# Two experts' inputs gathered at once, and the S5 tables' second part placed later, in a two-layer trunk on one core

## The chip, the core and the metric

The kernel runs on one core of a Trainium2 chip. The metric is the device time of one execution in microseconds, the median of several runs. TensorE (PE) multiplies matrices, VectorE (DVE), ScalarE (ACT) and GpSimd (POOL) work element by element, SyncE (SP) issues most DMA transfers. Each engine takes its instructions in the order in which they were written for it, and waits on semaphores for the others.

## The reference

Two layers over 256 latent and 256 context tokens of width 1024. Each layer has four parallel mixers (gated DeltaNet, S5, HGRN2, retention) between one input and one output projection; then layer 0 has a dense SwiGLU, layer 1 a mixture of eight experts of which each token takes two.

```python
def _swiglu(h, w1, w3, w2):
    return (jax.nn.silu(h @ w1) * (h @ w3)) @ w2

def _moe_swiglu(h, router, w1, w3, w2):
    ...
    logits = _f32(tok @ router)
    top_val, top_idx = lax.top_k(logits, TOP_K)
    gates = jax.nn.softmax(top_val, axis=-1)
    ...
    def expert_block(args):
        xblk, e = args
        return (jax.nn.silu(xblk @ w1[e]) * (xblk @ w3[e])) @ w2[e]
    yb = lax.map(expert_block, (xb, block_expert)).reshape(n_rows, -1)
    ...

def reference(x, c, ctx, ...):
    for layer in range(DEPTH):
        ...                      # the four mixers, w_out, layer norm
        x = _layer_norm(DEEPNORM_ALPHA * x + gt2 * ffn(x * (1.0 + sc2) + sh2), ln_g[layer, 1], ln_b[layer, 1])
```

The S5 mixer is a diagonal complex state space: lam_bar is raised to powers, and products of the powers with B and C make tables with which the scan is done in chunks.

## The kernel before

All is float32. A product of two float32 matrices is done as three products of parts (high times high, low times high, high times low): `whi` or `mhi` is a weight's high part, cast by ACT (L390), `wlo` or `mlo` the rest, subtracted by DVE (L305); `xh` and `xl` are the same of an input. Products are recorded at L373, the line of a helper.

**Order.** A framework places the instructions of each engine by a simulated timeline and by priorities. `context("B")` or `"A"` picks a scratch ring (k2B, k2A, k2P; each a ring of 128x512 tiles) and a priority; `high_priority(-2000)` moves work behind all other ready work. So the order is not written out, and an edit in one place may shift it in others.

**Stages.** By the trace's time: layer 0's start and S5 tables (0 to 140 us), its mixers (to 515), output projection and layer 1's S5 tables (to 610), the dense FFN (to 985), layer 1's mixers and the routing (to 1424), the experts (to 2456), the last norm.

**S5 tables.** `s5_tables` makes the powers and the state tables; `s5_out_tables` (L1343) the output tables: eight tiles Y of 128x512 a layer, each by two multiplications and a subtraction on DVE and one store by SP to a scratch in HBM. In layer 0 it is called in order, in layer 1 with priority -2000 beside the tables and the norm.

**Dense FFN.** A loop over f of 128-row pieces of the hidden width, with weights loaded by SP in tiles `wraw` of 128x1024.

**Experts.** `experts` (L1900) runs 8 experts x 7 steps. A step's `up` (L1824) takes four units, each a load `mraw` of 1 MB (128x2048) by SP, a cast `mhi` by ACT and a subtraction `mlo` by DVE, and does 48 products of 512 columns into two banks `psh`; SiLU and a multiplication make g (in k2P). `down` (L1844), one step later, transposes g (four transposes, L1848), splits it into `e_gh` and `e_gl`, and takes two more units for 24 products into `psy`. `mraw` has RAW = 8 buffers, `mhi` and `mlo` three each. That makes 8 x 7 x 6 = 336 units. After an expert's last step `scatter` adds its result to the tokens by products with `e_back`, in the next expert's first step. A loop for overflowing experts is built, but has no iterations here.

**The gather.** `gather` (L1765) makes the input of one expert: DVE compares positions with an index row to make `e_sel` (two tiles of 128x128 with one 1 per column), PE transposes these into `e_back`, and 32 products (8 pieces of the width, times two token halves, times high and low part `m_nh`, `m_nl`) select the expert's 128 tokens, 128 columns each. DVE scales and shifts by the modulation (L323), ACT makes `e_xh`, DVE `e_xl`. It is called at the start for expert 0 and in each expert's fifth step (c == 4) for the next.

## Time and profile before

| | us |
|---|---|
| median of 3 runs | 2485.07 (2484.03 to 2487.42) |
| the profiled execution | 2472.9 |
| its span, first to last instruction | 2470.8 |
| TensorE busy | 2262.0 (92%), mean granted clock 0.935 |
| DVE busy | 1735.4 (70%) |
| ACT busy | 1278.3 (52%) |
| POOL busy | 234.8 (10%) |
| read from HBM | 509.23 MB |

Busy times are of one execution. Products of TensorE overlap in the records, so their own durations are longer than the distance at which they start; where a cost is worked out, it is the distance of starts that counts. A table by stage gives, for each stretch, the length, the busy time and count of each engine (PE, PEld for weight loads, DVE, ACT, POOL), the granted clock of TensorE as a share of 2.4 GHz, the DMA's busy share and its GB/s.

### The profile page before, as it was taken

How to read it: one execution, taken by the hardware profiler on the slowest of the kernel's cores; microseconds unless marked ns; L12 is line 12 of the kernel's file. 1: busy time of each engine (PE TensorE's matmuls, PEld its weight loads, DVE VectorE, ACT ScalarE, POOL GpSimd, SP SyncE). 2: the span in 40 equal slices, each digit the busy share in tenths (PEclk: the TensorE clock that was granted, in tenths of full speed). 3: DMA queues.
4: the chain of work that ended last, by engine and by line, in shares of the span. 5: the costliest groups of instructions: out<-in, count | busy, mean ns of one | idle time of the engine just before them, and what ended most of it. 6: DMA issues, size and time to landing. Idle time of an engine off the chain costs nothing. (4 is left out here: it accounts for less than half of the span.)

```text
span 2470.8 us, 33235 instructions
## 1 busy us (share of the span) xinstructions
PE 2262.0 (92%) x12928; PEld 1777.8 (72%) x12928; DVE 1735.4 (70%) x2558; ACT 1278.3 (52%) x1483; POOL 234.8 (10%) x238
## 2 busy tenths in 40 slices
PE   4989989789999999799858799999999999999997
PEld 2767755565888887478747478787878788788885
DVE  8574657787444322464767599888888988889887
ACT  2634423325444422643524357676767667677775
POOL 0111331000111100002331000000000000010000
PEclk8989997789999999889978799999999999999998
DMA  7622144227223323742320669898998989899994
GB/s 296 220 90 81 61 163 137 90 89 273 94 95 102 124 94 131 241 147 81 106 75 27 227 246 353 323 347 335 344 347 336 353 320 363 318 369 341 364 356 164
DMA packets 123667, 532.75 MB, mean 216 GB/s; under 512 B 26096, under 2 KB 37360, under 8 KB 80112
## 3 DMA queue, kind: packets, MB, share of 16 engines
q1 hardware_dynamic: 96624, 511.74, 56.7%
q10 hardware_dynamic: 26880, 18.82, 2.6%
q8 instruction: 104, 1.70, 0.3%
q14 instruction: 59, 0.48, 0.1%
HBM read 509.23 MB, written 21.28 MB: 215 GB/s over the span
## 5 line engine op out<-in xcount | busy, mean ns | idle before, releaser
L305 DVE TENSOR_TENSOR mlo<-mraw,mhi 128x2048 fp32r<-128x2048 f32 x336 | 776.1, 2323 | 107.5 <-ACT mhi L390 105.8
L390 ACT CAST mhi<-mraw 128x2048 fp32r<-128x2048 f32 x336 | 639.1, 1906 | 216.3 <-PE psh L373 131.9
L373 PE MATMUL psh<-mlo,e_xh 128*128 128x512 f32 x896 | 357.9, 399 | 6.3 <-DVE mlo L305 6.3
L373 PE MATMUL psh<-mhi,e_xh 128*128 128x512 f32 x896 | 351.5, 395 | 7.8 <-ACT mhi L390 7.8
L373 PE MATMUL psh<-mhi,e_xl 128*128 128x512 f32 x896 | 351.6, 393 | 0.0
L390 ACT CAST whi<-wraw 128x1024 fp32r<-128x1024 f32 x142 | 145.9, 1028 | 375.0 <-PE psacc L373 346.8
L373 PE MATMUL psacc<-xh,whi 128*128 128x512 f32 (+2 forms) x784 | 314.1, 401 | 18.7 <-ACT k2P L329 8.4
L373 PE MATMUL psacc<-xl,whi 128*128 128x512 f32 (+2 forms) x784 | 309.3, 395 | 0.2 <-DVE xl L305 0.2
L373 PE MATMUL psacc<-xh,wlo 128*128 128x512 f32 (+2 forms) x784 | 306.8, 392 | 0.5 <-DVE wlo L305 0.4
L305 DVE TENSOR_TENSOR wlo<-wraw,whi 128x1024 fp32r<-128x1024 f32 x142 | 172.1, 1212 | 167.5 <-ACT whi L390 165.4
L373 PEld LDWEIGHTS psh<-mhi,e_xh 128*128 128x128 f32 x896 | 169.8, 189 | 46.1 <-ACT mhi L390 8.9
L373 PEld LDWEIGHTS psh<-mlo,e_xh 128*128 128x128 f32 x896 | 170.2, 190 | 43.2 <-DVE mlo L305 8.4
L373 PEld LDWEIGHTS psh<-mhi,e_xl 128*128 128x128 f32 x896 | 169.9, 190 | 34.4
L373 PEld LDWEIGHTS psacc<-xh,whi 128*128 128x128 f32 (+1 forms) x784 | 152.4, 195 | 56.3 <-ACT k2P L329 9.6
L373 PE MATMUL psy<-mlo,e_gh 128*128 128x512 f32 x448 | 176.9, 396 | 1.4 <-DVE mlo L305 1.4
L373 PEld LDWEIGHTS psacc<-xl,whi 128*128 128x128 f32 (+1 forms) x784 | 152.2, 194 | 34.3 <-issue 4.3
L373 PEld LDWEIGHTS psacc<-xh,wlo 128*128 128x128 f32 (+1 forms) x784 | 151.4, 193 | 35.0 <-issue 4.0
L373 PE MATMUL psy<-mhi,e_gl 128*128 128x512 f32 x448 | 173.7, 391 | 0.0
L373 PE MATMUL psy<-mhi,e_gh 128*128 128x512 f32 x448 | 159.9, 394 | 0.0
L305 POOL TENSOR_TENSOR e_xl<-k2B,e_xh 128x512 fp32r<-128x512 f32 x16 | 31.3, 1966 | 1024.5 <-ACT e_xh L1872 1024.5
L373 PEld LDWEIGHTS psy<-mlo,e_gh 128*128 128x128 f32 x448 | 84.4, 188 | 20.1 <-DVE mlo L305 2.9
L373 PEld LDWEIGHTS psy<-mhi,e_gh 128*128 128x128 f32 x448 | 84.3, 188 | 20.0 <-ACT e_gh L1851 1.5
(533 smaller groups left out, 3454.9 us busy)
## 6 DMA issues: line engine op xcount, KB each, us to landing
mraw<-in_moe_w_dram SPq DMA_DIRECT2D x336, 1024.0 KB, 6.5
wraw<-in_ada_w_dram SPq DMA_DIRECT2D x80, 512.0 KB, 4.4
wraw<-in_ffn_w_dram SPq DMA_DIRECT2D x60, 512.0 KB, 3.4
wraw<-in_w_feat_dram SPq DMA_DIRECT2D x44, 512.0 KB, 3.6
sraw<-in_ada_w_dram SPq DMA_DIRECT2D x16, 512.0 KB, 9.8
wraw<-in_w_out_dram SPq DMA_DIRECT2D x16, 512.0 KB, 3.9
wraw<-in_w_tok_dram SPq DMA_DIRECT2D x12, 512.0 KB, 3.4
s5c<-s5Y SPq DMA_DIRECT2D x16, 256.0 KB, 4.1
```

The lines of the kernel that those rows point to most:

```text
L305: (eng or self.V).tensor_tensor(out=out, in0=a, in1=b, op=op)
L373: self.T.matmul(out, lhsT, rhs, start=start, stop=stop, **k)
L390: self.S.copy(hi, raw)
```

## The change

Four things.

- `RAW` is 7 instead of 8.
- `s5_out_tables` is a generator that stops after each Y. Layer 0 runs it through after the first part's pool is left, in a pool of its own (`tabo`); layer 1 keeps it as `self.later` and takes one Y at each f > 2 of the FFN, with scratch from k2A.
- `gather` takes two experts: `e_sel` is two tiles of 128x256, a piece of the width is done for both at once, 32 products of 256 columns, two pieces to a bank instead of four. Scaling is done for both at once (128x256), ACT's copy and DVE's subtraction for each by itself. It is called at the start for experts 0 and 1, and in the fifth step of experts 1, 3 and 5 for the next two. `e_x` has three buffers, `e_back` three, `e_sel` one.
- `moe_begin` loads the norm's rows in halves into k2P by SP's queue instead of whole into an idle `e_x` by ACT's; its four operations become eight of half the width.

```diff
--- before.py
+++ after.py
@@ -229,7 +229,7 @@
 
 
 class Trunk:
-    RAW = 8
+    RAW = 7
 
     def __init__(self, ctx, tc, A, out, cat, pat, dbg=None):
         self.ctx, self.tc, self.nc = ctx, tc, tc.nc
@@ -1340,7 +1340,7 @@
         self.s5y2 = LC, Call
         return sr, sw, scm, sT
 
-    def s5_out_tables(self, scm):
+    def s5_out_tables(self, scm, ypool, cx):
 
         LC, Call = self.s5y2
         sh = [P, 4, 16, 8]
@@ -1349,13 +1349,14 @@
             lc = tuple(LC[:, c, gs, None, :].to_broadcast(sh) for c in range(2))
             cb = tuple(Call[:, c, gs, :, None].to_broadcast(sh) for c in range(3))
             for c, (a, b) in enumerate(((0, 1), (2, 0))):
-                Y = self.t("s5Y", [4, 16, 8])
-                with self.context("B"):
+                Y = self.t("s5Y", [4, 16, 8], pool=ypool)
+                with self.context(cx):
                     tmp = self.s2().rearrange("p (g h i) -> p g h i", g=4, h=16)
                 self.mul(Y, lc[0], cb[a])
                 self.mul(tmp, lc[1], cb[b])
                 self.sub(Y, Y, tmp)
                 self.nc.sync.dma_start(scm[g0 // 4][:, c * 512:c * 512 + 512], Y.rearrange("p g h i -> p (g h i)"))
+                yield
 
 
     def s5_phases(self, res):
@@ -1677,6 +1678,8 @@
             self.product([[A["ffn_w3"][f]]], self.xh, self.xl, NTOK, lambda i, acc: self.mul(h, h, acc))
             self.S.copy(gh[f], h)
             self.sub(gl[f], h, gh[f].bitcast(F32), eng=self.G)
+            if f > 2:
+                next(self.later, None)
         res = self.big.tile([P, KT, NTOK], F32, tag="xl", name=self.name("fres"))
         self.load_res(res, xt, (0, 1))
         pm = self.ps()
@@ -1762,38 +1765,40 @@
         self.nover = mt("nov", 1, dt=I32)
         self.V.tensor_copy(self.nover, cnt)
 
-    def gather(self, pos):
-
-
-        sel = self.t("e_sel", [2, P], F32R, bufs=2)
+    def gather(self, *pos):
+
+
+        n = len(pos)
+        sel = self.t("e_sel", [2, 2 * P], F32R)
         for b in range(2):
-            self.ts(sel[:, b], self.C("iota"), pos[b], ALU.is_equal)
+            for e in range(n):
+                self.ts(sel[:, b, e * P:(e + 1) * P], self.C("iota"), pos[e][b], ALU.is_equal)
         self32 = sel.bitcast(F32)
-        pt = self.ps()
-        for b in range(2):
-            self.T.transpose(pt[:, b * P:(b + 1) * P], self32[:, b], self.ident)
-        back = self.t("e_back", [2, P], F32R, bufs=2)
-        self.act(back.rearrange("p b t -> p (b t)"), pt[:, :256], AF.Copy)
-
-        if not self.ex[self.exi]:
-            self.ex[self.exi] = [self.t(f"e_x{c}{self.exi}", [KT, P], F32R) for c in "hl"]
-        xh, xl = self.ex[self.exi]
-        self.exi = 1 - self.exi
+        out = []
+        for e in range(n):
+            pt = self.ps()
+            for b in range(2):
+                self.T.transpose(pt[:, b * P:(b + 1) * P], self32[:, b, e * P:(e + 1) * P], self.ident)
+            back = self.t("e_back", [2, P], F32R, bufs=3)
+            self.act(back.rearrange("p b t -> p (b t)"), pt[:, :256], AF.Copy)
+            out.append((back, *(self.t("e_x" + c, [KT, P], F32R, bufs=3) for c in "hl")))
+
         A, B = self.AB[:, 0, 1], self.AB[:, 1, 1]
-        for k0 in range(0, KT, 4):
-            px = self.ps()
-            for k in range(4):
+        for k0 in range(0, KT, 2):
+            px = self.ps()[:, :2 * n * P].rearrange("p (k t) -> p k t", k=2)
+            for k in range(2):
                 for i, (nn, b) in enumerate((nn, b) for b in range(2) for nn in (self.nh, self.nl)):
-                    self.mm(px[:, k * P:(k + 1) * P], nn[:, b, (k0 + k) * P:(k0 + k + 1) * P], sel[:, b],
+                    self.mm(px[:, k], nn[:, b, (k0 + k) * P:(k0 + k + 1) * P], sel[:, b, :n * P],
                             start=(i == 0), stop=(i == 3))
             with self.context("B"):
-                x = self.s2().rearrange("p (k t) -> p k t", k=4)
-            for k in range(4):
-                self.ts(x[:, k], px[:, k * P:(k + 1) * P], A[:, k0 + k:k0 + k + 1], ALU.mult,
-                        B[:, k0 + k:k0 + k + 1], ALU.add)
-            self.S.copy(xh[:, k0:k0 + 4], x)
-            self.sub(xl[:, k0:k0 + 4], x, xh.bitcast(F32)[:, k0:k0 + 4])
-        return back, xh, xl
+                x = self.s2()[:, :2 * n * P].rearrange("p (k t) -> p k t", k=2)
+            for k in range(2):
+                self.ts(x[:, k], px[:, k], A[:, k0 + k:k0 + k + 1], ALU.mult, B[:, k0 + k:k0 + k + 1], ALU.add)
+            for e, (_, xh, xl) in enumerate(out):
+                xe = x[:, :, e * P:(e + 1) * P]
+                self.S.copy(xh[:, k0:k0 + 2], xe)
+                self.sub(xl[:, k0:k0 + 2], xe, xh.bitcast(F32)[:, k0:k0 + 2])
+        return out
 
     def raw_unit(self, src):
 
@@ -1884,18 +1889,21 @@
 
     def moe_begin(self):
 
-        rows = [self.t(f"e_x{c}1", [D]) for c in "hl"]
-        for j, nm in enumerate(("ln_g", "ln_b")):
-            self.nc.scalar.dma_start(rows[j], self.A[nm][1, 0:1, :].to_broadcast([P, D]))
 
         f = lambda t: t.bitcast(F32)
         one = f(self.t("e_gl", [4, P], F32R, bufs=2))[:, 0, 0:1]
         self.V.memset(one, 1.0)
         self.stt(self.macc, f(self.nh), one, f(self.nl), ALU.mult, ALU.add)
-        for b in range(2):
-            m = self.macc[:, b]
-            self.stt(m, m, ALPHA, rows[0], ALU.mult, ALU.mult)
-            self.stt(m, rows[1], ALPHA, m, ALU.mult, ALU.add)
+        for h in range(2):
+            sl = slice(h * 512, h * 512 + 512)
+            with self.context("P"):
+                g, s = self.s2(), self.s2()
+            for row, nm in ((g, "ln_g"), (s, "ln_b")):
+                self.nc.sync.dma_start(row, self.A[nm][1, 0:1, sl].to_broadcast([P, 512]))
+            for b in range(2):
+                m = self.macc[:, b, sl]
+                self.stt(m, m, ALPHA, g, ALU.mult, ALU.mult)
+                self.stt(m, s, ALPHA, m, ALU.mult, ALU.add)
 
     def experts(self, jobs, first=False):
 
@@ -1906,8 +1914,7 @@
         with self.tc.high_priority(-500):
             early = [self.unit(src, 4) for src in self.up_srcs(jobs[0][0], 0)[:3]]
         parts = self.up_parts(jobs[0][0], 0, 3)
-        self.ex, self.exi = [None, None], 0
-        x = {0: self.gather(jobs[0][1])}
+        x = dict(enumerate(self.gather(*(j[1] for j in jobs[:2]))))
         y, g, back = {}, {}, None
         for i in range(len(steps) + 1):
             if i < len(steps):
@@ -1915,8 +1922,8 @@
                 if i > 0:
                     parts = self.up_parts(jobs[n][0], c)
                 g[i] = self.up(chain(early if i == 0 else (), parts), x[n])
-                if c == NC - 3 and n + 1 < len(jobs):
-                    x[n + 1] = self.gather(jobs[n + 1][1])
+                if c == NC - 3 and n % 2 and n + 1 < len(jobs):
+                    x.update(enumerate(self.gather(*(j[1] for j in jobs[n + 1:n + 3])), n + 1))
             if i < 4 and first:
                 (self.route_gates, self.route_over, lambda: None, self.moe_begin)[i]()
             if back:
@@ -2011,9 +2018,11 @@
             self.enter("tab", "right")
             tables = self.s5_tables(l, y)
             self.leave("tab")
-            self.mx = y
-            self.s5_out_tables(tables[2])
-            self.leave("taby", "start")
+
+            y = self.enter("tabo", "right")
+            for _ in self.s5_out_tables(tables[2], y, "B"):
+                pass
+            self.leave("tabo", "taby", "start")
         self.enter("sP", "left")
         self.s5_begin(l, tables)
         self.enter("sW", "left")
@@ -2100,9 +2109,7 @@
         with self.context("B"):
             tables = self.s5_tables(1, y)
         self.leave("tab")
-        self.mx = y
-        with self.tc.high_priority(-2000):
-            self.s5_out_tables(tables[2])
+        self.later = self.s5_out_tables(tables[2], y, "A")
         for p in (0, 1):
             self.ada(1, p)
         self.enter("l1", "right")
```

Where instructions move, two places. DVE at layer 0's start, where the input's low part `xl` is made for the first projection. Before:

```order
L305 TENSOR_TENSOR s5Y_1139<-s5LC_834,s5C_700 128x512
L305 TENSOR_TENSOR s5res_768<-s5res_768,s5wtm_858 128x16x16
L305 TENSOR_TENSOR xl_196<-sx_200,xh_195 128x512
L305 TENSOR_TENSOR s5Y_1139<-s5Y_1139,k2B_1140 128x512
L305 TENSOR_TENSOR s5wtm_858<-s5res_768,s5wc_861 128x256
L305 TENSOR_TENSOR xl_196<-sx_200,xh_195 128x512
L305 TENSOR_TENSOR xl_196<-sx_210,xh_195 128x512
L305 TENSOR_TENSOR k2B_1158<-s5LC_834,s5C_700 128x512
L305 TENSOR_TENSOR xl_196<-sx_210,xh_195 128x512
L305 TENSOR_TENSOR s5res_768<-s5res_768,s5wtm_858 128x16x16
```

And now, from the same `xl` on:

```order
L305 TENSOR_TENSOR xl_196<-sx_200,xh_195 128x512 x2
L305 TENSOR_TENSOR xl_196<-sx_210,xh_195 128x512 x2
L305 TENSOR_TENSOR xl_196<-sx_220,xh_195 128x512 x2
L305 TENSOR_TENSOR xl_196<-sx_230,xh_195 128x512 x2
L305 TENSOR_TENSOR rlg_1434<-exp_1437,exi_1438 128x8
L321 TENSOR_SCALAR rlg_1434<-rlg_1434 128x8
L305 TENSOR_TENSOR wlo_319<-wraw_317,whi_320 128x1024
L305 TENSOR_TENSOR wlo_366<-wraw_364,whi_367 128x1024
L305 TENSOR_TENSOR s5Y_1130<-s5LC_834,s5C_700 128x512
```

The operations on s5Y and its scratch k2B stood between those on xl; now the first follows the weights' second wlo.

PE at the third change of expert (from the third to the fourth expert); psh is the fourth expert's first steps, psy the third expert's last and the fourth's first `down`, psA with k2P the transposes of g. Before:

```order
L1848 MATMUL psA_14645<-consts_74,k2P_14494 128x128 x4
L373 MATMUL psh_14690<-mhi_14694,e_xh_1958_12209 128x512
L373 MATMUL psy_2432_14643<-mhi_14657,e_gh_14650 128x512
L373 MATMUL psy_2432_14643<-mlo_14656,e_gh_14650 128x512
L373 MATMUL psy_2433_14644<-mhi_14657,e_gh_14650 128x512
L373 MATMUL psy_2433_14644<-mlo_14656,e_gh_14650 128x512
L1848 MATMUL psA_14767<-consts_74,k2P_14624 128x128 x4
L373 MATMUL psh_14690<-mlo_14693,e_xh_1958_12209 128x512
L373 MATMUL psh_14690<-mhi_14694,e_xl_1959_12210 128x512
L373 MATMUL psh_14690<-mhi_14694,e_xh_1958_12209 128x512
L373 MATMUL psh_14690<-mlo_14693,e_xh_1958_12209 128x512
```

And now:

```order
L373 MATMUL psy_2437_14594<-mlo_14606,e_gh_14600 128x512
L373 MATMUL psy_2437_14594<-mhi_14607,e_gl_14601 128x512
L373 MATMUL psy_2436_14593<-mhi_14625,e_gh_14600 128x512
L373 MATMUL psy_2437_14594<-mhi_14625,e_gh_14600 128x512
L1853 MATMUL psA_14717<-consts_74,k2P_14574 128x128 x4
L373 MATMUL psh_14640<-mhi_14644,e_xh_13135 128x512
L373 MATMUL psy_2436_14593<-mlo_14624,e_gh_14600 128x512
L373 MATMUL psy_2436_14593<-mhi_14625,e_gl_14601 128x512
L373 MATMUL psy_2437_14594<-mlo_14624,e_gh_14600 128x512
L373 MATMUL psy_2437_14594<-mhi_14625,e_gl_14601 128x512
L373 MATMUL psy_2436_14593<-mhi_14625,e_gh_14600 128x512
```

Before, both groups of transposes come within six rows, and 20 psy products of the first `down` follow after eleven of psh; now the psy products stand ahead of and around the second transposes.

## Rows read from the trace of the kernel before

**Rows 1.** The page's part 1, whole span: engine, busy us, share, instructions.

```profile
PE 2262.0 (92%) x12928; PEld 1777.8 (72%) x12928; DVE 1735.4 (70%) x2558; ACT 1278.3 (52%) x1483; POOL 234.8 (10%) x238
```

**Rows 2.** Table by stage, experts; columns: stretch, length, busy (count) per engine, clock, DMA, GB/s.

```profile
1420.00:1440.00 20.00, 17.40 (x79) 15.64 (x79) 16.67 (x95) 5.53 (x6) 0.00 (x0) 0.74 0.15 53
1440.00:1460.00 20.00, 20.00 (x91) 16.52 (x91) 17.94 (x11) 15.91 (x11) 0.00 (x0) 1.00 0.92 346
...
1480.00:1500.00 20.00, 19.99 (x103) 16.70 (x103) 20.00 (x22) 13.12 (x11) 0.00 (x0) 1.00 0.83 296
...
1580.00:1600.00 20.00, 16.91 (x65) 12.78 (x64) 14.53 (x11) 9.70 (x8) 0.00 (x0) 0.83 0.65 239
1700.00:1720.00 20.00, 16.36 (x73) 12.63 (x72) 18.46 (x14) 10.28 (x10) 3.16 (x2) 1.00 0.90 340
1840.00:1860.00 20.00, 16.88 (x62) 13.00 (x63) 13.85 (x10) 9.97 (x8) 0.00 (x0) 0.83 0.65 242
1960.00:1980.00 20.00, 17.37 (x67) 13.05 (x65) 17.79 (x13) 9.70 (x8) 3.15 (x2) 0.83 0.88 310
2100.00:2120.00 20.00, 16.56 (x73) 12.76 (x73) 15.10 (x12) 11.41 (x9) 0.00 (x0) 1.00 0.74 274
2220.00:2240.00 20.00, 19.74 (x90) 16.02 (x90) 19.70 (x14) 13.37 (x10) 3.65 (x2) 1.00 0.87 321
```

**Rows 3.** Timeline of PE at the first change of expert: start, duration, operation, idle before.

```profile
1580.18 0.60 PE L1848 MATMUL psA<-consts,k2P 128*128 128x128 f32 x4
1582.33 0.51 PE L373 MATMUL psh<-mhi,e_xh 128*128 128x512 f32 x1 [1.55 <-ACT mhi L390]
```

**Rows 4.** Waits, 1576 to 1600: engine and line, releaser: us, times, longest.

```profile
ACT mhi L390 <- PE psh L373: 7.8, 3, 5.1
```

**Rows 5.** Timelines of PE: first gather, second gather, a projection of 256 columns.

```profile
1425.29 0.41 PE L373 MATMUL psA<-e_sel,m_nl 128*128 128x128 f32 x1
...
1428.49 0.41 PE L373 MATMUL psA<-e_sel,m_nh 128*128 128x128 f32 x1
...
1485.83 0.27 PE L373 MATMUL psA<-e_sel,m_nh 128*128 128x128 f32 x1
1485.94 0.27 PE L373 MATMUL psA<-e_sel,m_nl 128*128 128x128 f32 x1
...
204.00 0.28 PE L373 MATMUL psacc<-whi,xl 128*128 128x256 f32 x1
204.12 0.28 PE L373 MATMUL psacc<-whi,xh 128*128 128x256 f32 x1
```

**Rows 6.** Timelines of DVE: the first gather, and the modulation of layer 0.

```profile
1428.31 1.36 DVE L323 TENSOR_SCALAR k2B<-psA,lnAB 128x128 f32<-128x128 f32 x4 [0.53 <-PE psA L373]
...
1430.36 0.69 DVE L305 TENSOR_TENSOR e_xl<-k2B,e_xh 128x512 fp32r<-128x512 f32 x1
...
60.38 2.66 DVE L323 TENSOR_SCALAR sx<-sx,sc1p,mods 128x256 f32<-128x256 f32 x8
```

**Rows 7.** Table by stage for layer 0's start, and the tile s5Y: count: minimum/median/maximum ns.

```profile
20.00:40.00 20.00, 6.28 (x41) 3.17 (x34) 19.83 (x114) 3.17 (x4) 0.00 (x0) 0.68 1.03 402
...
120.00:140.00 20.00, 10.22 (x44) 8.20 (x44) 17.39 (x23) 10.37 (x20) 0.00 (x0) 0.83 0.28 93
...
L305 DVE TENSOR_TENSOR s5Y<-s5LC,s5C x16: 680/684/1252, 26.2 to 596.9; 128x512 f32<-128x512 f32 x16
```

**Rows 8.** Timeline of PE at the hole in layer 0.

```profile
131.41 0.40 PE L373 MATMUL psacc<-xh,wlo 128*128 128x512 f32 x1
143.20 2.08 PE L373 MATMUL psP<-k2P,consts 128*128 128x512 f32 x2 [11.39 <-ACT k2P L329]
```

**Rows 9.** Table by stage: layer 1's table stretch, and the dense FFN.

```profile
540.00:560.00 20.00, 20.00 (x95) 15.96 (x95) 20.00 (x67) 6.09 (x12) 0.00 (x0) 1.00 0.30 104
...
620.00:720.00 100.00, 100.00 (x442) 82.81 (x442) 42.57 (x47) 43.41 (x57) 16.35 (x9) 1.00 0.31 97
```

**Rows 10.** The page's part 6: DMA issues, count, KB each, us to landing.

```profile
mraw<-in_moe_w_dram SPq DMA_DIRECT2D x336, 1024.0 KB, 6.5
```

## The prediction

> **What bounds the kernel now.** I read the page's busy shares first, then tables by stage, then the order of events at the places that the diff touches. TensorE is busy 2262.0 of 2470.8 us [rows 1], so the question at each stage is what keeps TensorE from work, or how much work it has. The experts' stage (1424 to 2456 us) is TensorE's in its steady stretches: 20.00 of 20 us busy with some 90 products, VectorE just behind it at 17.94 [rows 2]. Five of the seven changes from one expert to the next break this: the windows from 1580, 1700, 1840, 1960 and 2100 hold 65, 73, 62, 67 and 73 products. The sixth (2220) holds 90, so the stall is no necessity. The timeline of the first shows why [rows 3]: four transposes, 1.55 us of waiting for ACT's mhi, one product of psh, four of psy, four transposes, and a wait for the next unit. ACT itself had waited up to 5.1 us for TensorE's psh [rows 4]: mhi and mlo have three buffers, and a new unit is cast only when an old one has been used up.
>
> In layer 0, DVE is full at 20 to 40 us (19.83 of 20), and TensorE has a hole at 120 to 140 (10.22 of 20) [rows 7]: it waits 11.39 us for ACT's k2P in front of one psP product [rows 8]. In layer 1's table stretch both TensorE and DVE are full; in the FFN only TensorE is, DVE 42.57 of 100 [rows 9].
>
> **The gather.** Before, each expert takes 32 products of 128 columns. At full clock they start 0.11 us apart; in the first gather, in a window with a mean granted clock of 0.74 [rows 2], 15 of them span 3.20 us, 0.213 each [rows 5]. So 32 x 0.213 + 7 x 32 x 0.11 = 6.8 + 24.6 = 31.4 us. After, a pair takes 32 products of 256 columns, four times in all. No gather of 256 columns is in the trace; the projections have 256-column products of the same kinds, 0.12 apart [rows 5]. Bounds: 0.12 (the projection's) and 0.22 (twice the 128-column start). I take 0.12, a product of that size, and for the first pair at low clock twice it, as the 128-column rows have it: 32 x 0.24 + 3 x 32 x 0.12 = 7.7 + 11.5 = 19.2. That is **-12 us**; at 0.22 it is 32 x 0.44 + 96 x 0.22 = 35.2, a loss of 4.
>
> What goes with it on DVE: before, per expert and per half of the k range, four scalings (1.36) and one subtraction (0.69) [rows 6], so 4.1 per expert, 8.2 a pair. After, a pair has eight scalings of 128x256 (2.66 for eight [rows 6]) and eight subtractions of 128x256, between half of 0.69 and the whole of it, 2.8 to 5.5. So 5.5 to 8.2, not more than before in sum, but in one step instead of two, and DVE was full at 20.00 of 20 in the stretch with one gather [rows 2]. That puts up to 4 us more on DVE in each of three steps, and one such excess ahead of the first expert's products, half of which the three mhi/mlo buffers and the step's slack should take: **+3 us** (0 to +12). moe_begin's four operations become eight of half the size, with no gather beside them any more: 0.
>
> The Trainium skill ("TensorE: Matmul & The Clock Gate", section "Back-to-back issue gap") gives N/2.4 + 2.5 ns as the gap of a single product, so 56 and 109 ns, by which two of 128 columns cost what one of 256 does and the gather would save 0.3 us (an estimate from that page). The rows speak against it, 0.11 and 0.12. The same page's section "LDWEIGHTS" gives P/1.2 ns for a weight load, 107 ns for 128 columns, which fits a start of 0.11 set by the load and not by the columns.
>
> **The experts' order.** Where the products stand is decided anew. In the order before, a change of expert reads as in the excerpt: all of the new expert's first products stand ahead of most of the old one's psy products, which hold the mhi/mlo buffers that the next products wait for. In the order after, at the second to seventh change, the psy products stand ahead of it, as they do before at the sixth, which loses nothing. Only the first keeps the old pattern. What a stall costs: a full window has 90 products, 0.222 us each, so the five lack 25, 17, 28, 23 and 17 products [rows 2], or 5.6, 3.8, 6.2, 5.1 and 3.8 us. The last four go: -18.9. The second change has a pattern that neither trace shows exactly; bounds 0 and its old 3.8. I take **-18** in all. The cover of this gain is that nothing stands right behind TensorE: DVE has 17.94 of 20, and the DMA must deliver 336 units in some 30 us less.
>
> **RAW 8 to 7, and the ln rows.** A buffer is held from issue until mlo is made. 336 units in 1032 us are 3.07 us each; eight buffers make a round of 24.6 us. Landing takes 6.5 [rows 10], cast and subtraction some 4.5, so 13 us to spare, and 10 with seven. The four ln rows go through SP's queue among these loads; the second pair waits for k2P buffers that TensorE's transposes free, and the raw loads queue behind. That is one step, 3 us, out of 10 to spare: **0**. If the cover were gone it would be up to 3 us, once.
>
> **Layer 0.** The eight Y tiles are three DVE operations each of 0.68 us [rows 7]. In the order before, eight of these stand ahead of the modulation that the first projection needs; in the order after none does, and the excerpt shows the same behind it, among the xl. DVE is full there, some 0.6 us each: up to 4.8 us earlier; **-3**, since weights still have to arrive (0 to -5). They move to where the projections run and DVE has gaps. The hole [rows 8] ended when ACT's k2P did, whose DVE operations stood behind the S5 scan. In the order after they stand ahead of the scan, and more projections stand ahead of the waiting psP product. What is late next is the S5 scan itself and the DVE work after it, so I keep two thirds of the 11.39: **-7** (-14, with the low clock behind it, to +10 if a hole opens elsewhere).
>
> **Layer 1's tables.** All eight Y tiles go into the FFN, one at each f from 3 to 10: three DVE operations, 2 us, into a stage where DVE is idle over half [rows 9]. Hidden; if the k2A ring held up the FFN's own tile it would be 2 us for each of eight. In the table stretch DVE loses 16 us of work, but TensorE is just as full there [rows 9], so it is worth little: **-2** (0 to -6). The SP queue's Y stores now stand among the FFN's weight loads, which have time. Layer 1's mixers are shuffled a little, with no term that I can name: 0, give or take 6.
>
> **Sum.** -12 + 3 - 18 - 3 - 7 - 2 = -39 us against the profiled execution's 2472.9 (span 2470.8), so 2434. The median of the runs shown is 2485.07, 12 above that execution; the same difference put on it gives **2446**.
>
> **Rivals.**
> *The stalls come back.* The three mhi/mlo buffers are as before, and where 32 products of 256 columns come at once DVE must make eight scalings in their shadow. If each removed stall is replaced by one near a gather, the gather's -9 and the layers' -12 stay: -21, 2464. For: DVE at 20.00 [rows 2]. Against: the sixth change, gather-free in either order, and four places gathered at instead of eight.
> *The mixers give it back.* Layer 0's S5 scan is now later; if TensorE finds a hole of the old size behind the scan, +11 with the low clock after it instead of -7: -21, 2464. If layer 1 opens another like it, with some 5 us of low clock behind it, -5, 2480.
> *The gather saves nothing,* 256 columns costing 0.22, +4 instead of -12: -23, 2462.
> *The loads become the pace (slower).* Loads already move 346 GB/s and more in the steady stretch (the table's last column). If the eight outstanding buffers set this rate, seven give 7/8 of it: 352 MB at 303 GB/s are 1163 us for the stage instead of 1032, +131, and the gather's and the order's gains are lost: 2600. In between, it decides from the point where a load takes over 16 us to land. Against: 6.5 [rows 10], two or three loads in flight on average, not eight.
> That Y's move does nothing is part of the forecast (-2).
>
> **How the numbers follow.** Forecast 0.58, with a range of its own from 2430 to 2462. Stalls back 0.15, mixers give it back 0.12, gather nothing 0.03; the second mixers case, within 5 us of before, 0.06; slower, by the loads or a larger hole, 0.06. A measurement of this kernel can tell about 0.2%, 5 us, from no change. So faster 0.88, same 0.06, slower 0.06. The range, 2424 to 2474, takes in the forecast's and the first two rivals, and leaves out the last cases and the tails of the first.
>
> **What would show it.** Gather: e_sel products 128x256 start 0.12 apart, 128 of them. Stalls: the windows at the second to seventh change hold some 90 products, the first still about 65. Loads: mhi never waits for a DMA. Layer 0: the first psacc some 3 us earlier, no wait of 11 us for k2P. Layer 1: FFN products without gaps though s5Y stands in DVE's rows. Wrong would be: a TensorE wait of over 3 us for e_xh, e_xl or mlo near the pair's gather; DVE over 19.5 of 20 through whole steps; a new hole at low clock between 140 and 300 us or between 1000 and 1420.

## The result, and the profile after

The changed kernel takes 2453.65 us (2449.76 to 2460.26, 4 runs) against 2486.24 of before (2484.03 to 2498.0, 4 runs). The ratio is 0.9879, with a 95% interval of 0.9848 to 0.991: about 30 us less. The forecast was 2446, between 2424 and 2474.

The profiled executions say something else at first sight: 2470.8 to 2458.5 us of span, 12 us. This page shows TensorE's share nearly unchanged, and the loads a little slower to land than in [rows 10].

```profile
PE 2248.6 (91%) x12800; PEld 1766.6 (72%) x12800; DVE 1723.6 (70%) x2546; ACT 1276.9 (52%) x1499; POOL 239.3 (10%) x238
...
mraw<-in_moe_w_dram SPq DMA_DIRECT2D x336, 1024.0 KB, 7.2
```

The span must be cut in two. The experts' stage begins with the first transpose of e_sel and ends with the norm's first statistics on m_acc. The views of these two tiles give the first and last start (in us, behind the durations in ns); in the changed kernel:

```profile
L1781 PE MATMUL psA<-consts,e_sel x16: 272/273/473, 1445.6 to 2118.2; 128*128 128x128 f32 x16
```

```profile
L1578 DVE BATCH_NORM_STATS2 lnst<-m_acc x4: 678/680/696, 2445.5 to 2447.3; 128x6 f32<-128x512 f32 x4
```

So it begins at 1445.6 and ends at 2445.5, 999.9 us. Before:

```profile
L1774 PE MATMUL psA<-consts,e_sel x16: 272/273/477, 1423.9 to 2250.6; 128*128 128x128 f32 x16
L1577 DVE BATCH_NORM_STATS2 lnst<-m_acc x4: 677/678/695, 2457.9 to 2459.7; 128x6 f32<-128x512 f32 x4
```

It began at 1423.9 and was 1034.0 us long. The stage became 34 us shorter, and all that lies ahead of it took 22 us longer. The experiments had to say whether these 22 us are the change's or the execution's.

In the stage, the table at the seven changes from one expert to the next, to be held against the five short windows of [rows 2] (columns as there):

```profile
1600.00:1620.00 20.00, 17.86 (x66) 13.87 (x67) 13.18 (x9) 9.96 (x9) 0.00 (x0) 0.83 0.63 238
1720.00:1740.00 20.00, 18.93 (x85) 15.30 (x86) 18.02 (x13) 12.84 (x10) 3.13 (x1) 1.00 0.95 339
1840.00:1860.00 20.00, 19.66 (x90) 15.80 (x89) 19.67 (x14) 14.01 (x10) 5.78 (x2) 1.00 0.97 324
1960.00:1980.00 20.00, 19.68 (x88) 15.63 (x87) 19.66 (x16) 13.57 (x11) 6.45 (x2) 1.00 0.94 345
2080.00:2100.00 20.00, 19.66 (x88) 15.61 (x87) 19.66 (x15) 13.45 (x11) 6.46 (x2) 1.00 0.98 338
2200.00:2220.00 20.00, 19.67 (x88) 15.64 (x87) 18.98 (x14) 13.14 (x10) 6.45 (x2) 1.00 0.98 358
2320.00:2340.00 20.00, 19.66 (x87) 15.59 (x86) 18.65 (x14) 13.27 (x10) 6.48 (x2) 1.00 0.98 363
```

Only the first is still short, with 66 products; the second has 85, the others about 90. The timeline of the first is that of [rows 3] again: transposes, a wait for mhi, transposes, a wait for mlo.

```profile
1598.52 0.60 PE L1853 MATMUL psA<-consts,k2P 128*128 128x128 f32 x4
1600.67 0.50 PE L373 MATMUL psh<-mhi,e_xh 128*128 128x512 f32 x1 [1.55 <-ACT mhi L390]
...
1602.76 1.12 PE L1853 MATMUL psA<-consts,k2P 128*128 128x128 f32 x4 [0.39 <-DVE k2P L305]
1604.95 0.80 PE L373 MATMUL psh<-mlo,e_xh 128*128 128x512 f32 x1 [1.08 <-DVE mlo L305]
```

The first gather, to be held against [rows 5]:

```profile
1446.37 0.41 PE L373 MATMUL psA<-e_sel,m_nl 128*128 128x256 f32 x1
1446.59 0.41 PE L373 MATMUL psA<-e_sel,m_nh 128*128 128x256 f32 x1
1446.80 0.41 PE L373 MATMUL psA<-e_sel,m_nl 128*128 128x256 f32 x1
...
1449.10 0.28 PE L373 MATMUL psA<-e_sel,m_nl 128*128 128x256 f32 x1
1449.22 0.29 PE L373 MATMUL psA<-e_sel,m_nh 128*128 128x256 f32 x1
1449.34 0.28 PE L373 MATMUL psA<-e_sel,m_nl 128*128 128x256 f32 x1
```

At the low clock of its start, products of 256 columns begin 0.213 us apart, as those of 128 did; at full clock 0.12. From its first product to the first psh product behind it, the gather of two experts takes 5.4 us; that of one took 7.0 before.

Layer 0's first projection starts at 64.20 instead of 64.14, and DVE makes mods, the modulation, at 57.35 instead of 57.44. Before (columns: start, duration, operation, idle before):

```profile
57.44 0.17 DVE L305 TENSOR_TENSOR mods<-psP,params 128x16 f32<-128x16 f32 x1
...
64.14 1.20 PE L373 MATMUL psacc<-xh,whi 128*128 128x512 f32 x2
```

And now DVE, which waits, with PE, for ACT's xh:

```profile
30.91 1.89 DVE L305 TENSOR_TENSOR k2B<-s5LC,s5C 128x512 f32<-128x512 f32 x3
...
57.35 0.17 DVE L305 TENSOR_TENSOR mods<-psP,params 128x16 f32<-128x16 f32 x1
...
64.18 2.50 DVE L305 TENSOR_TENSOR xl<-sx,xh 128x512 fp32r<-128x512 f32 x4 [1.87 <-ACT xh L476]
```

```profile
64.20 1.22 PE L373 MATMUL psacc<-xh,whi 128*128 128x512 f32 x2 [2.75 <-ACT xh L476]
```

Of the Y tiles' eight operations ahead of mods, three are still there, multiplications into the scratch k2B at 30.91, which the excerpt of the change does not show.

The hole of [rows 8] is gone as one wait and back as several:

```profile
114.21 0.77 PE L373 MATMUL psacc<-xh,whi 128*128 128x512 f32 x1 [6.03 <-ACT k2P L329]
...
124.89 0.77 PE L373 MATMUL psacc<-xh,whi 128*128 128x512 f32 x1 [2.54 <-ACT k2P L331]
...
140.67 0.40 PE L373 MATMUL psacc<-xh,whi 128*16 128x512 f32 x1 [2.87 <-DVE k2P L317]
```

The FFN with the Y tiles in it, for [rows 9]: DVE has more to do, TensorE is full as before.

```profile
620.00:720.00 100.00, 100.00 (x437) 82.67 (x436) 56.85 (x68) 43.10 (x58) 12.18 (x9) 0.99 0.36 116
```

### The profile page after: what moved, and what is told of

It is laid out like the page before. It is cut to its first block, busy times and chain, and to the rows that moved or that the text cites. A ratio compares the mean times of both kernels' runs of the same rounds, so it can differ in the third digit from the quotient of the medians.

```text
span 2458.5 us, 32948 instructions
## 1 busy us (share of the span) xinstructions
PE 2248.6 (91%) x12800; PEld 1766.6 (72%) x12800; DVE 1723.6 (70%) x2546; ACT 1276.9 (52%) x1499; POOL 239.3 (10%) x238
## 5 line engine op out<-in xcount | busy, mean ns | idle before, releaser
L305 DVE TENSOR_TENSOR mlo<-mraw,mhi 128x2048 fp32r<-128x2048 f32 x336 | 768.1, 2307 | 74.3 <-ACT mhi L390 72.4
L373 PE MATMUL psh<-mlo,e_xh 128*128 128x512 f32 x896 | 352.9, 394 | 1.8 <-DVE mlo L305 1.8
L373 PE MATMUL psacc<-xh,whi 128*128 128x512 f32 (+2 forms) x784 | 312.7, 400 | 40.9 <-ACT k2P L329 15.9
L305 POOL TENSOR_TENSOR e_xl<-k2B,e_xh 128x512 fp32r<-128x512 f32 x16 | 43.9, 2758 | 977.8 <-ACT e_xh L1877 977.8
```

What stands on the lines that cost most here:

```text
L305: (eng or self.V).tensor_tensor(out=out, in0=a, in1=b, op=op)
L373: self.T.matmul(out, lhsT, rhs, start=start, stop=stop, **k)
```

## The experiments

All kernels at a glance. The stage's start and length are read as above. "Layer 0" is the time from the first gXs product to the first hea product in layer 0 (the tile views give both first starts: before 307.8 and 399.7), "layer 1" from that layer's first s5H product to its first gXs product. Ratios are to before, with the 95% interval.

| kernel | tables placed | stage starts | stage | layer 0 | layer 1 | ratio |
|---|---|---|---|---|---|---|
| before | before | 1423.9 | 1034.0 | 92.0 | 140.0 | |
| before_again | before | 1429.9 | 1033.7 | 92.4 | 140.0 | 0.9998 (0.9974 to 1.0023) |
| after | both new | 1445.6 | 999.9 | 99.6 | 146.0 | 0.9879 (0.9848 to 0.991) |
| after_again | both new | 1448.5 | 999.9 | 104.7 | 146.6 | 0.9873 (0.9835 to 0.9912) |
| tables_only | both new | 1455.4 | 1034.8 | 107.8 | 149.2 | 1.0031 (1.0003 to 1.0058) |
| l0_old | layer 1 new | 1439.8 | 999.2 | 90.9 | 145.2 | 0.9886 (0.9844 to 0.9929) |
| l1_old | layer 0 new | 1438.9 | 1000.0 | 104.2 | 140.1 | 0.9862 (0.9806 to 0.9918) |
| gather_only | before | 1428.8 | 999.2 | 92.4 | 141.3 | 0.9844 (0.9798 to 0.989) |
| raw7 | before | 1442.8 | 1026.1 | 95.3 | 139.9 | 0.996 (0.9935 to 0.9985) |
| pair128 | both new | 1448.8 | 1028.4 | 103.3 | 148.2 | 1.0031 (1.0003 to 1.006) |
| late_before | before | 1434.4 | 1011.4 | 96.0 | 142.2 | 0.9918 (0.9894 to 0.9942) |
| late_gather | before | 1441.6 | 995.8 | 92.1 | 143.8 | 0.9857 (0.9825 to 0.989) |
| late_pair128 | before | 1433.2 | 1014.9 | 92.6 | 143.8 | 0.99 (0.9861 to 0.994) |
| late_first | before | 1433.2 | 992.0 | 95.3 | 140.0 | 0.9815 (0.9783 to 0.9846) |

The stage's length is the sharp number: kernels with the same order in it agree within 1.2 us. The part ahead varies far more, from 1423.9 to 1442.8 among the eight profiles with both tables as before.

### The same kernels once more

before_again, no edit:

> The kernel before, unchanged, once more. The two profiles put the changed kernel 21.7 us later at the start of the experts' stage and 34.3 us shorter in it, while the medians differ by 32.6 us in all. Theory (the part ahead of the experts differs from execution to execution by more than the change moves it): this profile's experts' stage starts some 10 us or more away from the 1424 us of the first, its length stays within 3 us of the first's 1034, and the ratio is 1.000. Rival (the 21.7 us are the change's own): the stage starts again within 5 us of 1424.

after_again, no edit:

> The changed kernel, unchanged, once more. Theory (the part ahead varies): the experts' stage, which began at 1446 us, begins some 10 us earlier or more, its length is again within 3 us of 1000. Rival (the change itself costs 21.7 us ahead): it begins within 5 us of 1446 again. Ratio to before 0.985 to 0.991 either way.

Before began its stage at 1429.9 (6 us later), after at 1448.5 (3 later). So the part ahead does vary, but the changed kernel's stays some 19 us later: the first theory falls for most of the 22 us.

### The gather alone, the tables alone

gather_only, against before: `gather` and `moe_begin` of the change, and

```diff
-    RAW = 8
+    RAW = 7
```

> The kernel before with the pairwise gather, its moe_begin and RAW 7, and the S5 tables as before. The order of TensorE in the experts' stage is that of the changed kernel. Theory (the whole gain is in the experts' stage): that stage is 34 us shorter than before's and the rest as before, so about -34 us, 2452. Rival (the forecast's layer terms are real too): the gain is 12 us smaller than the changed kernel's, about -21, 2465. Second rival (the tables' move costs 20 us ahead of the experts, as the first two profiles read): this is faster than the changed kernel by 10 us or more.

tables_only, against before: the generator, its calls in layer 0 and in the FFN, and not the rest.

```diff
-            self.mx = y
-            self.s5_out_tables(tables[2])
-            self.leave("taby", "start")
+            y = self.enter("tabo", "right")
+            for _ in self.s5_out_tables(tables[2], y, "B"):
+                pass
+            self.leave("tabo", "taby", "start")
...
-        with self.tc.high_priority(-2000):
-            self.s5_out_tables(tables[2])
+        self.later = self.s5_out_tables(tables[2], y, "A")
```

> The kernel before with the S5 tables' second part placed as in the changed kernel, gather and RAW 8 as before; the order of TensorE in the experts' stage is before's, five stalls included. Theory (the tables' move is worth nothing in time): within 5 us of before. Rival (the forecast: start -3, hole -7, layer 1 -2): -12 us, 2474. Second rival (the two profiles: it costs up to 20 us): +10 us or more, 2495.

The gather alone has the whole of the stage's gain (999.2) and starts it like before (1428.8): 2446.0 us, 0.9844. The tables alone have before's stage (1034.8) and start it at 1455.4: 1.0031, slower by 1 to 14 us with the interval. So the forecast's layer terms, -12 us, have the wrong sign. Which stretch it is shows in the columns "layer 0" and "layer 1"; the windows in layer 0, of before_again and then of tables_only:

```profile
312.00:332.00 20.00, 16.12 (x519) 9.39 (x515) 7.78 (x19) 4.82 (x12) 2.63 (x4) 0.91 0.82 265
332.00:352.00 20.00, 19.38 (x184) 10.85 (x179) 8.09 (x18) 10.32 (x22) 12.90 (x15) 1.00 0.64 224
```

```profile
312.00:332.00 20.00, 13.10 (x412) 5.91 (x408) 5.37 (x12) 3.68 (x8) 1.95 (x3) 0.83 0.76 251
332.00:352.00 20.00, 15.81 (x186) 9.44 (x181) 3.57 (x7) 6.25 (x16) 1.05 (x2) 0.75 0.68 221
```

The same stretch, the chain of small products of gated DeltaNet, beside the products for later parts of layer 0's own modulation: TensorE is busy 28.9 of 40 us instead of 35.5, DVE 8.9 instead of 15.9.

### Which of the two placements

l0_old, against after:

```diff
-            y = self.enter("tabo", "right")
+            self.mx = y
             for _ in self.s5_out_tables(tables[2], y, "B"):
                 pass
-            self.leave("tabo", "taby", "start")
+            self.leave("taby", "start")
```

> The changed kernel, but layer 0's Y tiles are placed as before (in the first part's pool, no pool of their own); layer 1's are in the FFN. Two profiles of before and one with the gather alone reach the experts' stage at 1424 to 1430 us, three with the tables moved at 1446 to 1455. Theory (layer 0's placement costs these 20 us, by an order of the mixers that it shifts): the stage starts at 1425 to 1432, total like the gather alone, 2446. Rival (layer 1's placement costs them): it starts at 1445 or later, total like the changed kernel, 2457. In between, both. The experts' stage is 1000 us long in any case.

l1_old, against after:

```diff
-        self.later = self.s5_out_tables(tables[2], y, "A")
+        self.mx = y
+        with self.tc.high_priority(-2000):
+            for _ in self.s5_out_tables(tables[2], y, "B"):
+                pass
+        self.later = iter(())
```

> The changed kernel, but layer 1's Y tiles are made with the tables as before, at priority -2000; layer 0's are in their own pool. Theory (layer 0's placement costs 20 us): the experts' stage starts at 1445 us or later, total 2457. Rival (layer 1's): it starts at 1425 to 1432, total 2446. In the FFN, DVE has 16 us less to do than with the tiles in it, and the FFN is as long, 367 us.

Both, and each in its own layer. Layer 0's stretch takes 90.9 to 96.0 us in the nine profiles with layer 0's tables as before and 99.6 to 107.8 in the five with them moved, 93 and 104 on the mean. Layer 1's takes 139.9 to 143.8 in nine without and 145.2 to 149.2 in five with the tables in the FFN, 141 and 147. The stage starts at 1433.5 on the mean of the eight profiles with both tables as before, and at 1449.6 on that of the four with both moved. This distance of 16 us is about the sum of the two stretches; the stretches between differ by up to 4 us either way and cancel. Some 5 of the 16 lie in which execution was profiled: the four stood 4.5 us above their kernels' medians on the mean, the eight 0.6 below. The ratios can't tell l0_old and l1_old from the changed kernel; tables_only's puts the two together at 1 to 14 us. The rows of layer 0 show where the chain is held back. DVE in tables_only, the operation of ACT that it waits for, and DVE in before_again:

```profile
348.74 1.23 DVE L305 TENSOR_TENSOR wlo<-wraw,whi 128x1024 fp32r<-128x1024 f32 x1 [14.04 <-ACT whi L390]
...
356.03 0.42 DVE L305 TENSOR_TENSOR gvn<-gu,psB 128x256 f32<-128x256 f32 x1 [2.76 <-PE psB L373]
```

```profile
347.67 1.04 ACT L390 CAST whi<-wraw 128x1024 fp32r<-128x1024 f32 x1 [4.92 <-DMA wraw<-in_w_feat_dram]
```

```profile
339.75 0.42 DVE L305 TENSOR_TENSOR gvn<-gu,psB 128x256 f32<-128x256 f32 x1 [9.63 <-ACT gvt L329]
...
344.21 2.10 DVE L305 TENSOR_TENSOR wlo<-wraw,whi 128x1024 fp32r<-128x1024 f32 x1 [0.55 <-ACT whi L390]
```

With layer 0's tables moved, the cast and the subtraction of a weight of the next projection (whi on ACT, wlo on DVE) stand ahead of the chain's gvt and gvn; otherwise they stand behind. In all fourteen profiles this cast begins 30 to 35 us after the first gXs product, once its load has landed. So the chain's gvn, at 26.5 to 32.4 us in the nine profiles, comes at 37.4 to 43.6 in the five, where DVE waits 12.0 to 14.6 us for whi. Some 4 of these 12 us are lost before, since the chain's products of gyf with grw begin at 21.3 to 25.4 us instead of 16.4 to 20.9. From gvn to the first hea product it is 62 to 68 us in all. No run moves this cast alone, so that is read from the rows and not tested. In layer 1 the distance is there early: the psP product from which the gates are made starts 19.0 to 20.6 us after the first s5H product in the nine, 25.0 to 26.9 in the five. What holds it back was not isolated and stays open.

### Seven load buffers

raw7, against before:

```diff
-    RAW = 8
+    RAW = 7
```

> The kernel before with RAW 7 alone. Gather as before. The order of TensorE has the short group of psy products ahead of the second transposes at three changes of expert instead of five, since the planner times the loads anew. Theory (a stall is a matter of that order, some 5 us each; seven buffers cost nothing): the experts' stage is 1034 - 2 x 5 = 1024 us long, no product waits for a load, total about -10 us. Rival (the loads become the pace with seven): the stage is longer than 1034, up to 1160, and mhi or mlo waits for DMAs. Second rival (the stalls do not come from the order): five windows of 62 to 73 products as before, 1034.

The stage is 1026.1 us, 8 shorter, and no product waits for a load. The windows at the first four changes of expert:

```profile
1600.00:1620.00 20.00, 16.98 (x63) 13.08 (x64) 13.77 (x10) 10.04 (x8) 0.00 (x0) 0.83 0.67 247
1730.00:1750.00 20.00, 17.36 (x74) 13.35 (x72) 15.14 (x12) 11.73 (x9) 0.00 (x0) 0.91 0.78 286
1860.00:1880.00 20.00, 17.78 (x66) 13.74 (x67) 13.21 (x9) 9.81 (x9) 0.00 (x0) 0.83 0.65 247
1980.00:2000.00 20.00, 18.67 (x84) 14.62 (x83) 18.20 (x13) 12.48 (x9) 3.91 (x2) 1.00 0.86 315
```

The fourth, 67 products before [rows 2], now has 84, and no stall is left at the fifth, which had 73: taking a buffer away made the kernel faster, 0.996 (0.9935 to 0.9985), because the planner's times moved and with them the order. The loads-become-the-pace rival is dead.

### Order and width, one at a time

late_before, against before: the scatter's products of an expert one step later, nothing added or removed.

```diff
-            if back:
+            if back and i > 0 and steps[i - 1][1] == 1:
                 back()
```

> The kernel before with the same one edit: scatter one step later; gather for one expert, RAW 8, tables as before. The order has psy ahead at all seven changes. Theory (order alone, apart from the gather): the five stalls, 28 us by the gaps between products, go; the stage is 1006 us long instead of 1034, total -28, 2455. Rival (the pairwise gather removes the stalls by having less for VectorE to do at the changes): the stage stays above 1025.

```profile
1580.00:1600.00 20.00, 20.00 (x90) 16.14 (x89) 20.00 (x15) 13.68 (x11) 4.62 (x2) 1.00 0.96 325
1700.00:1720.00 20.00, 20.00 (x91) 16.16 (x90) 19.51 (x15) 14.43 (x11) 4.61 (x2) 1.00 0.89 322
1820.00:1840.00 20.00, 18.84 (x85) 15.15 (x84) 19.22 (x15) 13.14 (x11) 6.43 (x2) 1.00 0.87 331
1960.00:1980.00 20.00, 20.00 (x91) 16.45 (x91) 18.71 (x12) 14.36 (x10) 0.00 (x0) 1.00 0.91 325
2080.00:2100.00 20.00, 18.83 (x85) 15.18 (x84) 19.43 (x13) 12.85 (x10) 5.21 (x2) 1.00 0.96 330
```

With the gather of before and its eight buffers, the five stalls are gone and 22.3 us with them. That is what shows the order to be their cause. At five changes a gap of 1.55 us came in, where a product waits for POOL's e_xl (columns as in the timelines above):

```profile
1829.63 0.39 PE L373 MATMUL psA<-e_xh,e_back 128*128 128x512 f32 x1
1831.18 0.51 PE L373 MATMUL psA<-e_xl,e_back 128*128 128x512 f32 x1 [1.16 <-POOL e_xl L305]
```

Without these it would have been about the 28.6 us that the gaps of the five stalls sum up to in the trace of before (6.4, 4.7, 6.7, 6.3 and 4.5 over the usual distance). Some 2 us of the first, third and fourth of these are not waiting but TensorE's low clock behind the waits: eight to ten products of 512 columns start 0.43 us apart there instead of 0.227. The granted clock behind the first stall of before (table by stage):

```profile
1587.40:1590.30 2.90, 2.90 (x8) 2.27 (x7) 0.52 (x1) 0.00 (x0) 0.00 (x0) 0.50 0.94 381
```

pair128, against after (late_pair128: the same on late_gather):

```diff
-                for i, (nn, b) in enumerate((nn, b) for b in range(2) for nn in (self.nh, self.nl)):
-                    self.mm(px[:, k], nn[:, b, (k0 + k) * P:(k0 + k + 1) * P], sel[:, b, :n * P],
-                            start=(i == 0), stop=(i == 3))
+                for e in range(n):
+                    es = slice(e * P, (e + 1) * P)
+                    for i, (nn, b) in enumerate((nn, b) for b in range(2) for nn in (self.nh, self.nl)):
+                        self.mm(px[:, k, es], nn[:, b, (k0 + k) * P:(k0 + k + 1) * P], sel[:, b, es],
+                                start=(i == 0), stop=(i == 3))
```

> The changed kernel, but the products of the pairwise gather are of 128 columns, 64 a pair instead of 32 of 256; all else the same. TensorE's order then has stalls at three changes of expert instead of one. Measured in the changed kernel: 256-column starts 0.12 apart at full clock, and 0.213 at low clock, as the 128-column ones. Theory (half of the gain is the width, half the order): 64 products at 0.111 are 7.1 us a pair instead of 3.9, for four pairs +12 to +14, and two more stalls of 5 each: the experts' stage is some 1023 us long. Rival (the width saves nothing, since VectorE's part of the gather is what is waited for): 1010, the two stalls alone. Second rival (the stalls are no matter of the order): 1013.

The stage is 1028.4, 28 us longer than the changed kernel's: 5 more than expected. Three of its changes of expert stall, two more than in the changed kernel, and gaps of 1.5 us stand at three places, also two more: that is where 3 of the 5 are.

late_gather is gather_only with late_before's edit:

> The kernel with the pairwise gather alone (S5 tables as before), and in it the scatter's products of an expert come one step later, in the next expert's second step instead of its first. Its TensorE order has psy products ahead of the next transposes at all seven changes of expert; no operation is added or removed. Theory (the stalls come from that order): the first change's stall of 6.9 us and 1.5 us at the second go, the experts' stage is 991 us long instead of 999, total about 2438. Rival (a stall belongs to the first change, where the buffers are not yet in step): 999 as before.

995.8, not 991: the first change's stall is gone, but six gaps of 1.57 us came in at the others. The total, 2452.39, can't be told from gather_only's.

late_pair128:

> The changed kernel's pairwise gather with 128-column products (64 a pair), S5 tables as before, scatter one step later. The same as late_gather but for the width of the gather's products. Theory (width is worth what the starts say): 64 x 0.111 = 7.1 us instead of 32 x 0.12 = 3.8 for three pairs, and some 64 x 0.213 or less for the first instead of 5.4: the stage is 12 to 18 us longer than late_gather's, 1003 to 1009. Rival (VectorE's scalings set the gather's time): within 4 us of late_gather's.

1014.9 against 995.8 with no stall by order in either: the width is worth 19 us, a little above the expected 12 to 18. Some 7 of them lie in the first gather, mostly at the low clock, where 64 products take 13.7 us and 32 of twice the width 6.3. The rival, that DVE's scalings set the gather's time, is out.

### A faster kernel

late_first, against gather_only:

```diff
-            if back:
+            if back and i != NC + 1:
                 back()
```

> The pairwise gather alone (S5 tables as before), the scatter one step later after the first expert only. The order has psy ahead of the transposes at all seven changes, and the six later changes are as in the kernel with the gather alone, without the 1.57 us gaps ahead of e_xl's products that the later scatter brought there. Theory: the gather-alone stage of 999.2 us less the first change's stall of 6.9 and the second's 1.4 is 991; the total some 8 us under the gather alone's 2446, 2438, faster than the changed kernel by 15 to 20. Rival (the whole gain of late_gather over the gather alone, 3.4 us, is all there is at the first change): 996.

The windows around the first change of expert and at the second:

```profile
1560.00:1580.00 20.00, 20.00 (x91) 16.36 (x89) 18.27 (x13) 15.51 (x13) 4.49 (x2) 1.00 0.99 376
1570.00:1590.00 20.00, 20.00 (x90) 16.22 (x89) 19.51 (x15) 14.24 (x11) 4.60 (x2) 1.00 0.90 344
1690.00:1710.00 20.00, 19.70 (x88) 15.60 (x88) 18.97 (x14) 13.28 (x11) 6.52 (x2) 1.00 0.98 364
```

No stall is left, the stage takes 992.0 us, and the kernel 2439.75 (2433.27 to 2443.18, 6 runs), 0.9815 (0.9783 to 0.9846): below the kernels before and after, by some 45 and 15 us. Against gather_only's 2446.0 the stage is 7 us shorter (8 were expected), while the intervals of the two ratios overlap.

## Why the prediction came out

The time lay in the range and the sign was right, but two errors cancelled in part: the experts' stage gave 34 us where -27 stood in the sum, and the layers took time where -12 stood. How much they took depends on the measure: 4 us by the changed kernel's own ratio (30 us less in all, 34 in the stage), 8 by that of tables_only (1 to 14), 16 by the starts of the stage in the profiles. That the forecast of 2446 comes within 8 us of 2453.65 is luck as far as it rests on this cancelling.

- **Gather's products, -12: right in mechanism, mis-sized.** 0.12 at full clock was exact. At low clock 0.24 was taken, twice the full-clock distance; it was 0.213, and the clock rose within the gather. So 31.4 became 5.4 + 3 x 3.84 = 16.9, -14.5. Where the clock rose later, the first gather took about 1 us more (l0_old, gather_only).
- **DVE's excess, +3: not there.** No product waits for a pair's e_xh or e_xl in the changed kernel; a wait of 1.9 us for ACT's k2P in the first expert's first step (at 1461.8) is new. late_gather is 15.6 shorter than late_before, which differs by gather, moe_begin and RAW: the whole product term and 1 us more.
- **Stalls, -18: right, also in place.** The first stayed, the second kept a gap of 1.5, five are clean. By the gaps it is 28.6 before and 6.5 + 1.4 after, -20.7; counting products in 20 us windows had missed what lies past a window's edge. -14.5 - 20.7 = -35.2, measured -34.1; the new wait at 1461.8 goes against it.
- **RAW and ln rows, 0: right.** Seven buffers alone cost nothing, and gained by the order.
- **Layer 0's start, -3: wrong.** What stood ahead of mods on DVE was taken for what it waited for. Of eight operations five went, not all eight as was read from the order; the other table work closed up, and the psP products that mods needs end at 56.4 in the changed kernel, so little more than 1 us was to be had. mods came 0.1 us earlier and ACT's sx, behind it, 0.6, but two copies of s5wt now stand ahead of ACT's first xh.
- **The hole, -7: wrong.** It was split over four waits; the first gXs product came at 307.3 instead of 307.8. On the mean it came at 310.7 in the five profiles with layer 0's tables moved and at 313.1 in the nine others, within their spread: some 2 us for layer 0's two terms together, not 10. "What is late next" was asked and answered too kindly.
- **Layer 1, -2 and "mixers 0, give or take 6": the first right, the second the step that failed.** From the first product on lr, which opens layer 1's table stretch, to the first of the FFN it is 80 to 82 us instead of 83 to 84, and the FFN is as long with the Y tiles in it. But the moved tables changed the order of both mixers, far from where the edit stands, and that costs 11 us in layer 0's DeltaNet stretch and 6 in layer 1's (in the profiles). In layer 0, by the rows, the step that was not seen is mainly a weight's cast and subtraction that now stand ahead of the chain's gvn. The rival "the mixers give it back" was near the truth for the layers, with the place wrong.

The Trainium skill ("TensorE: Matmul & The Clock Gate", section "Back-to-back issue gap") gives N/2.4 + 2.5 ns for a single product by itself, and says that at small N it counts too little, since it leaves out the weight loads. The trace agrees: products of 128 columns, each with a load of its own, start 0.11 us apart and not 0.056, and where the formula would have let the pairing save 0.3 us (an estimate from it), the width is worth 19 (late_pair128 against late_gather).

## What to carry to other kernels

Where a tight ring feeds the engine that sets the pace, look at the order of the products that free its buffers: a change of loop that lets the next loop's products overtake them cost some 5 us each time here, and moving one small step of work mended it without removing any. A saving on an engine that is full counts only if the next wait in the row is shown to be earlier; read who is waited for after it. And where a planner orders the work, measure each part of a change alone: the parts that move only order can cost, far away, what the others gain.

## What the runs showed of the hardware

At the low level of the clock (1.2 GHz, granted clock 0.50 in the first gather) products of 128 and of 256 columns start 0.213 us apart; at the high one (2.4 GHz, 1.00) 0.11 and 0.12. So up to 256 columns the width costs nearly nothing here. Products of 512 columns start 0.43 and 0.227 us apart at the two levels. The part ahead of the experts varied by some 6 us between two executions of the same kernel (1423.9 and 1429.9), while the experts' stage, 1034.0 and 1033.7, did not.
